# Sample attention of a streaming encoder: queries as weights, 32 columns per pair of heads, in four column groups

## The chip, the cores and the metric

The kernel runs on one core of a Trainium2 chip. The metric is the device time of one execution in microseconds. The time before the change is 3033.25 us, the median of 3 runs (3031.68 to 3037.04). The engines are called PE (TensorE's matmuls), PEld (its weight loads, which overlap the matmuls), DVE (VectorE), ACT (ScalarE), POOL (GpSimd) and SP (SyncE, which issues most of the DMAs).

## What is computed

The reference is one layer of a streaming encoder for a prompt of 2048 frames and for 8 samples (streams) of 16 new frames each. The layer has a mixer (attention and convolution side by side), a cross-attention into 256 memory tokens and a feed-forward network. The change touches the attention of the samples only:

```python
# per sample: 16 queries, 8 heads of 64; keys and values: 256 cached rows and the 16 new ones
s = jnp.einsum("bqhd,bkhd->bhqk", qc, kc, preferred_element_type=jnp.float32) * scale + bias
s = jnp.where(valid[None, None, None, :], s, NEG_INF)
p = jax.nn.softmax(s, axis=-1)
return jnp.einsum("bhqk,bkhd->bqhd", p.astype(vc.dtype), vc)
```

The bias is a learned one per head and relative distance. With 8 heads of 16 queries a sample has 128 rows of scores, each of 272 keys. The two heads 2c and 2c+1 are a pair; their 2 x 64 channels are the 128 channels of block c, for c = 0 to 3.

## The kernel before

The program is built phase by phase: memory keys and values, input projection with the convolution, attention, output projection, cross-attention, feed-forward. A scheduler orders the instructions of each engine from a simulated timeline, so the order on an engine is not that of the code; each engine runs its own list in order. All matmuls of the prompt split an operand into a high and a low part (float32r, types `fp32r` in the profile); those of the samples are plain float32.

`attention()` runs over 128 units (h, t): head h = 0 to 7, tile t = 0 to 15 of 128 queries. In step i it issues the scores of unit i (L861, up to 640 keys, PSUM buffer "s", two of them), then the transposes of the weights of unit i - 4 (L878, PSUM buffer "t", three of them), and every fourth step the values of a quad of units (L891, PSUM buffer "o", a single one). DVE adds the bias and finds the minimum (L793), ACT takes the exponential (L795), ACT and DVE evict the transposes as high and low part (L879 and L880), and ACT and DVE evict the values (L895 and L897).

Between these steps one sample is worked off per head, `sample(s)` with s = h. It is a generator, and `next(fill)` lets it go on by one piece at i = 2, 4, ..., 14 of a head's 16 units, and at every unit at the end of the last head. Its pieces are:

- The DMA loads of the cached keys (L800) and values (L802, "vc", two buffers) and of the new values (L804).
- Two times four transposes of the keys (L812) and their eviction by ACT into kt (L813), each time a piece; then POOL's copy of the 16 new keys into kt (L815), a piece of its own.
- The scores: DVE copies the queries into qb (L820), one of two zeroed tiles of 128 x 4 x 160. Read as 640 columns, its 128-column slice c holds the 32 query columns of pair c at columns 32c to 32c + 31 and zeros elsewhere. Four matmuls (L826), each with such a slice as weights and 272 keys as moving columns, accumulate into the same 128 x 272 of PSUM. Softmax follows (L793, L795, L829, and L830 on POOL).
- Three transposes of the weights (L835), the last of only 16 keys, and their eviction by ACT (L837, L838).
- The values: per pair c, two matmuls with 128 rows of cached values as weights (L844) and one with the 16 new rows (L845); 128 weight columns each time, and 32 moving columns, the weights of the pair's heads. The result is 128 channels x 32, of which DVE copies the two needed parts into attS (L847, L848).

`att_pools()` places the tiles in fixed arenas; fa, fb, sbF and sbR are arenas in SBUF, which the profile and the order show as flexb, sbf, sbr and sbx.

Of the kernel before, what the change touches and what calls it, by code (L numbers as in the profile page):

```python
# [8 lines left out]
F32 = mybir.dt.float32  # L9
# [8 lines left out]
P = 128  # L18
# [12 lines left out]
DEC_S = 16  # L31
# [105 lines left out]
class Build:  # L137
# [611 lines left out]
    def att_pools(self):  # L749
        sbF, sbR, fa, fb = self.sbF, self.sbR, self.fa, self.fb  # L750
        self.attp = (Region().lay(sbF, 34.5, ("kc", 4, 2), ("kt", 4.25, 1), ("pp", 1.5, 1), ("vn", 2, 1))
                     .at("z", 2.5, (fa, [24]), (fb, [0, 2.5, 5]), (fa, [9, 11.5, 14, 16.5]))
                     .lay(fb, 7.5, ("vc", 4, 2), ("nmx", 0.03125, 12), ("sm", 0.03125, 2))
                     .lay(fa, 0, ("qbd", 2.5, 2), ("otmp", 2, 1), ("bs", 1.0625, 1)).lay(fa, 19, ("bt", 2.5, 2))
                     .lay(sbR, 0, ("q20", 8, 1), ("k20", 8, 1), ("kl0", 8, 1), ("q21", 8, 1), ("k21", 8, 1), ("kl1", 8, 1),
                          ("v20", 8, 1), ("ph1", 10, 1), ("pl1", 10, 1), ("v21", 8, 1))
                     .lay(sbR, 88, ("ph0", 10, 1), ("pl0", 10, 1)))
# [25 lines left out]
    def attention(self):  # L783
        nc, A = self.nc, self.A
        ps, pool = self.ps, self.attp
# [4 lines left out]
        def softmax_band(ps, w, bias, sm):  # L790
            z = self.t(pool, [P, W5], F32, "z", 6)
            nmx = self.t(pool, [P, 1], F32, "nmx", 12)
            nc.vector.tensor_tensor_reduce(out=z[:, :w], in0=ps, in1=bias, scale=-1.0, scalar=3e38,  # L793
                                           op0=ALU.add, op1=ALU.min, accum_out=nmx[:, :])
            nc.scalar.activation(z[:, :w], z[:, :w], AF.Exp, bias=nmx[:, :], scale=-1.0, accum_out=sm)  # L795
            return z

        def sample(s):
            kc = self.t(pool, [P, 2, 512], F32, "kc", 2)
            nc.sync.dma_start(kc[:, :, :], A["cache_att_k"][s].rearrange("(b p) d -> p b d", p=P))  # L800
            vc = self.t(pool, [P, 2, 512], F32, "vc", 2)
            nc.sync.dma_start(vc[:, :, :], A["cache_att_v"][s].rearrange("(b p) d -> p b d", p=P))  # L802
            vn = self.t(pool, [DEC_S, 512], F32, "vn", 2)
            nc.sync.dma_start(vn[:, :], self.vsamp[s * DEC_S:(s + 1) * DEC_S, :])  # L804
            yield
            kt = self.t(pool, [P, 4, PAST + DEC_S], F32, "kt", 1)
            for c2 in range(0, 4, 2):
                pt = self.t(ps_t, [P, 2, 2, P], F32, "t")
                for c in range(2):
                    for b in range(2):  # L810
                        cc = slice((c2 + c) * P, (c2 + c + 1) * P)
                        nc.tensor.transpose(pt[:, c, b, :], kc[:, b, cc], self.ident[:, :])  # L812
                nc.scalar.copy(kt[:, c2:c2 + 2, :PAST].rearrange("p c (b k) -> p c b k", k=P), pt[:, :, :, :])  # L813
                yield
            nc.gpsimd.tensor_copy(kt[:, :, PAST:], self.ksamp[:, :, s * DEC_S:(s + 1) * DEC_S])  # L815
            yield
            qb = qbds[s % 2]
            for o in range(2):
                rr = slice(o * DH, (o + 1) * DH)
                nc.vector.tensor_copy(qb[rr, :, o * DEC_S:(o + 1) * DEC_S],  # L820
                                      self.qsamp[rr, :, s * DEC_S:(s + 1) * DEC_S])
            qb = qb[:, :, :].rearrange("p c x -> p (c x)")
            n = PAST + DEC_S
            ps = self.t(ps_s, [P, 2, 512], F32, "s")[:, 0, :n]
            for c in range(4):
                nc.tensor.matmul(ps, qb[:, c * P:(c + 1) * P], kt[:, c, :], start=c == 0, stop=c == 3)  # L826
            sm = self.t(pool, [P, 1], F32, "sm", 2)
            z = softmax_band(ps, n, bs[:, :], sm[:, :])
            nc.vector.reciprocal(sm[:, :], sm[:, :])  # L829
            nc.gpsimd.tensor_scalar(z[:, :n], z[:, :n], sm[:, :], None, ALU.mult)  # L830
            yield
            pt = self.t(ps_t, [P, 3, P], F32, "t")
            for b in range(3):
                w = P if b < 2 else DEC_S
                nc.tensor.transpose(pt[:w, b, :], z[:, b * P:b * P + w], self.ident[:, :])  # L835
            pp = self.t(pool, [P, 3, P], F32, "pp", 1)
            nc.scalar.copy(pp[:, :2, :], pt[:, :2, :])  # L837
            nc.scalar.copy(pp[:DEC_S, 2, :], pt[:DEC_S, 2, :])  # L838
            yield
            po = self.t(ps_o, [P, 4, 32], F32, "o")  # L840
            for c in range(4):
                cc, hc = slice(c * P, (c + 1) * P), slice(c * 32, (c + 1) * 32)
                for b in range(2):
                    nc.tensor.matmul(po[:, c, :], vc[:, b, cc], pp[:, b, hc], start=b == 0, stop=False)  # L844
                nc.tensor.matmul(po[:, c, :], vn[:, cc], pp[:DEC_S, 2, hc], start=False, stop=True)  # L845
            ss = slice(s * DEC_S, (s + 1) * DEC_S)
            nc.vector.tensor_copy(self.attS[:DH, :, ss], po[:DH, :, :DEC_S])  # L847
            nc.vector.tensor_copy(self.attS[DH:, :, ss], po[DH:, :, DEC_S:])  # L848
# [53 lines left out]
        bs = self.t(pool, [P, PAST + DEC_S], F32, "bs")  # L902
# [1 line left out]
            nc.sync.dma_start(bs[h * DEC_S:(h + 1) * DEC_S, :], toep[h][:DEC_S, PAST:2 * PAST + DEC_S])  # L904
        qbds = []
        for _ in range(2):
            qb = self.t(pool, [P, 4, P + 2 * DEC_S], F32, "qbd")
            nc.gpsimd.memset(qb[:, :, :], 0.0)
            qbds.append(qb)
        fill = iter(())  # L910
# [5 lines left out]
        for i in range(n + LV + 1):  # L916
            if i < n:
                h, t = units[i]
                if t == 0:
                    fill = sample(h)  # L920
                if t == 6 and h + 1 < H:
                    heads[h + 1] = self.head_tiles(h + 1)
                    self.head_load(h + 1, heads[h + 1], 0, NPT)
                zq[h, t] = scores(heads[h], t, self.sums[:, t, h:h + 1])
            u = i - LT
            if 0 <= u < n:
                h, t = units[u]
                quads[u // 4] = transp({x: zq.get((h, x)) for x in range(t - t % 4, t + 1)}, t, quads.get(u // 4))
            u = i - LV
            if 0 <= u < n and u % 4 == 3:  # L930
                h, t = units[u]
                values(h, heads[h], t - 3, quads.pop(u // 4))
            if i % NPT and (i % 2 == 0 or i > SLAST):
                next(fill, None)
            if i == n - NPT:
                self.selectors()
            if i in WEIGH:
                for _ in self.weigh(WEIGH.index(i), ps_t, "t"):
                    pass
            if i in (n - 13, n - 11, n - 9, n - 7):  # L940
                next(self.wo_load)
# [760 lines left out]
```

## Time and profile before

| | |
|---|---|
| median of 3 runs | 3033.25 us |
| the profiled execution | 3033.59 us |
| its span, first to last instruction | 3031.8 us |
| its mean granted TensorE clock | 0.987 |
| attention (643 to 917 us) | 274 us, PE busy 261.3, DVE 201.9, ACT 209.6, POOL 23.0 |
| samples' scores, L826 | 64 PE instructions, first at 662.2, last at 906.9 us |
| samples' values, L844 and L845 | 128 and 64 PE instructions, first at 682.5, last at 916.5 us |

The time of the profiled execution holds its span and about 2 us around it. A row of the trace names the engine, the line, the operation, the tile written and those read, then the shapes; `128*128 128x272 f32` on PE is 128 rows by 128 columns of weights and a moving operand of 272 columns. PE's durations run from start to end of one instruction and overlap the next, so the cost of an instruction in a row of many is the distance between starts. Clock 1.00 is full speed.

### The profile page before, as it was taken

What the parts mean: (1) busy time and instruction counts of PE and PEld (TensorE: products, weight loads), DVE (VectorE), ACT (ScalarE), POOL (GpSimd) and SP (SyncE); (2) the same over time, 40 slices, a digit from 0 to 9 for tenths busy, and PEclk for the clock granted to TensorE, in tenths of its full rate; (3) what the DMA queues carried; (4) which work ended last, traced back from release to release, by engine and by line L of the source; (5) the groups of instructions that cost most, each with busy time, mean ns of one, the idle gap of its engine ahead of it and who ended that gap; (6) DMA issues with size and microseconds to landing.
All of it is one profiled execution on the core that took longest, in us unless ns stands there. A gap on an engine that the chain in (4) does not pass through costs nothing.

```text
span 3031.8 us, 45992 instructions
## 1 busy us (share of the span) xinstructions
PE 2949.8 (97%) x16924; PEld 2715.4 (90%) x16924; DVE 2138.1 (71%) x3077; ACT 1357.7 (45%) x2718; POOL 1397.0 (46%) x1304
## 2 busy tenths in 40 slices
PE   8999999979999999999999999999999999999998
PEld 8999999969997888787888999999999999888786
DVE  6696895957775466535357887888788998656655
ACT  4545454757784345323234333433334444433433
POOL 0267495710012234325356655555555776424413
PEclk9999999989999999999999999999999999999999
DMA  8635255557753556324246433544334446756654
GB/s 300 245 110 188 87 161 163 169 142 182 170 145 134 176 183 227 125 66 144 78 167 216 138 133 119 180 161 160 139 130 153 145 139 208 255 172 208 222 196 163
DMA packets 196429, 500.08 MB, mean 165 GB/s; under 512 B 18981, under 2 KB 82989, under 8 KB 187875
## 3 DMA queue, kind: packets, MB, share of 16 engines
q1 hardware_dynamic: 185883, 461.09, 47.3%
q0 software_dynamic: 10320, 36.05, 3.1%
q8 instruction: 133, 2.18, 0.3%
q14 instruction: 93, 0.76, 0.1%
HBM read 365.97 MB, written 141.81 MB: 167 GB/s over the span
## 4 chain that ended last, share of the span: by engine, by line
PE 40%; DMA 3%; DVE 3%; POOL 2%; issue 1%; ACT 1%; SPq 0%; DVEq 0%; POOLq 0%; ACTq 0%
PE psb L285 13%; PE psb L284 13%; PE psb L283 13%; DMA sbf<-in_w_down_dram 1%; PE psb L291 1%; DMA sbf<-x 1%; POOL sbf L1553 1%; DVE sbr L1614 1%; PE psb L1408 1%; DMA sbf<-hn 0%; DVE sbr L1431 0%; POOL sbf L340 0%; DMA hn<-sbf 0%; DVE flexb L1493 0%; DMA sbf<-in_w_gate_dram 0%
## 5 line engine op out<-in xcount | busy, mean ns | idle before, releaser
L283 PE MATMUL psb<-sbr 128*128 128x384 f32 (+3 forms) x2808 | 943.3, 337 | 4.4 <-ACT sbr L1613 1.4
L284 PE MATMUL psb<-sbr 128*128 128x384 f32 (+3 forms) x2356 | 806.8, 343 | 2.7 <-DVE sbr L320 2.4
L285 PE MATMUL psb<-sbr 128*128 128x512 f32 (+3 forms) x1848 | 633.2, 344 | 3.5 <-DVE sbr L1614 3.4
L283 PEld LDWEIGHTS psb<-sbr 128*128 128x128 f32 x2808 | 531.2, 189 | 34.4 <-ACT sbr L1613 2.8
L285 PE MATMUL psb<-sbr,sbx 128*128 128x384 f32 (+2 forms) x1484 | 477.8, 323 | 0.0
L284 PEld LDWEIGHTS psb<-sbr 128*128 128x128 f32 x2356 | 445.8, 189 | 29.8 <-DVE sbr L320 2.7
L285 PEld LDWEIGHTS psb<-sbr 128*128 128x128 f32 x1848 | 348.1, 189 | 33.3 <-DVE sbr L1614 6.6
L291 PE MATMUL psb<-sbr 128*128 128x512 f32 x1200 | 296.1, 395 | 6.4 <-DVE sbr L1019 1.7
L1431 DVE TENSOR_TENSOR sbr<-sbf,sbr 128x512 fp32r<-128x512 f32 x258 | 263.1, 1023 | 39.7 <-ACT sbr L1430 38.8
L1430 ACT CAST sbr<-sbf 128x512 fp32r<-128x512 f32 x258 | 159.3, 620 | 276.9 <-PE psb L284 231.0
L285 PEld LDWEIGHTS psb<-sbr,sbx 128*128 128x128 f32 x1484 | 281.5, 190 | 0.2
L291 PEld LDWEIGHTS psb<-sbr 128*128 128x128 f32 x1200 | 222.8, 189 | 52.9 <-DVE sbr L1019 1.9
L523 DVE SCALAR_TENSOR_TENSOR psb<-sbf,psb 128x768 f32<-128x768 f32 (+1 forms) x290 | 264.3, 911 | 6.2
L1614 DVE TENSOR_TENSOR sbr<-sbf,sbr 128x384 fp32r<-128x384 f32 (+1 forms) x231 | 170.8, 762 | 94.0 <-ACT sbr L1613 92.1
L278 POOL TENSOR_TENSOR sbx<-sbf,sbr 128x1024 fp32r<-128x1024 f32 x60 | 151.6, 2529 | 80.7 <-ACT sbr L277 77.2
L1613 ACT CAST sbr<-sbf 128x384 fp32r<-128x384 f32 (+1 forms) x231 | 111.0, 497 | 168.3 <-PE psb L284 153.7
L1553 POOL TENSOR_TENSOR sbf<-sbf 128x512 f32<-128x512 f32 x77 | 108.0, 1407 | 167.9 <-DMA sbf<-in_w_down_dram 166.1
L533 POOL TENSOR_TENSOR flexb<-flexb,flexb 128x128 f32<-128x128 f32 (+1 forms) x180 | 169.4, 941 | 22.3 <-ACT flexb L532 12.8
L283 PE MATMUL psb<-sbr,sbx 128*128 128x384 f32 (+1 forms) x524 | 170.6, 327 | 1.6 <-ACT sbx L1430 0.9
L1430 ACT CAST sbx<-sbf 128x512 fp32r<-128x512 f32 x153 | 94.7, 621 | 162.4 <-PE psb L284 150.6
L1431 DVE TENSOR_TENSOR sbx<-sbf,sbx 128x512 fp32r<-128x512 f32 x153 | 152.3, 997 | 15.9 <-ACT sbx L1430 15.5
L277 ACT CAST sbr<-sbf 128x1024 fp32r<-128x1024 f32 x98 | 102.7, 1051 | 107.2 <-PE psb L284 57.6
(336 smaller groups left out, 6246.9 us busy)
## 6 DMA issues: line engine op xcount, KB each, us to landing
af<-flexb SPq DMA_DIRECT2D x33, 1344.0 KB, 6.0
sbf<-in_w_down_dram SPq DMA_DIRECT2D x154, 256.0 KB, 3.8
sbf<-af SPq DMA_DIRECT2D x90, 384.0 KB, 3.9
sbf<-in_w_gate_dram SPq DMA_DIRECT2D x66, 512.0 KB, 3.4
sbf<-in_w_up_dram SPq DMA_DIRECT2D x66, 512.0 KB, 3.4
sbf<-x SPq DMA_DIRECT2D x49, 512.0 KB, 3.9
sbf<-in_w_in_dram SPq DMA_DIRECT2D x48, 512.0 KB, 4.1
sbr<-ks SPq DMA_DIRECT2D x28, 512.0 KB, 10.2
```

The source lines that it names most:

```text
L278: self.lo_engine.tensor_tensor(lo[:, :], wf[:, :], hi[:, :].bitcast(F32), ALU.subtract)
L283: nc.tensor.matmul(ps, lh, rh, start=start, stop=False, **kw)
L284: nc.tensor.matmul(ps, lh, rl, start=False, stop=False, **kw)
L285: nc.tensor.matmul(ps, ll, rh, start=False, stop=stop, **kw)
L291: nc.tensor.matmul(y[o], l, r[:, o * 512:(o + 1) * 512], start=start and x == 0, stop=stop and x == 2)
L523: nc.vector.scalar_tensor_tensor(acc if w < CW - 1 else o, src(w), cwt[:, j, w:w + 1], acc, ALU.mult, ALU.add)
L533: nc.gpsimd.tensor_tensor(o, o, v, ALU.add)
L1430: nc.scalar.copy(hs[j][:, :], src[j])
L1431: nc.vector.tensor_tensor(ls[j][:, :], src[j], hs[j][:, :].bitcast(F32), ALU.subtract)
L1553: nc.gpsimd.tensor_tensor(acc[:, :], acc[:, :], q[:, :], ALU.add if s > 0 else ALU.subtract)
L1613: nc.scalar.copy(ch[:, m], a[:, x, m])
L1614: nc.vector.tensor_tensor(cl[:, m], a[:, x, m], ch[:, m].bitcast(F32), ALU.subtract)
```

## The change

The samples' attention is written anew in three places. The scores use as weights only the 32 query columns of a pair (qb shrinks to 128 x 4 x 32), and each of the four matmuls writes its own 32 partitions of PSUM, 32c to 32c + 31, without accumulating over pairs. The values turn the operands round: the weights are the 32 columns of pp, the moving operand is the 128 channels of the pair, and each pair writes its own 32 partitions of a 128 x 128 tile; the blocks b of keys are the outer loop, the pairs the inner one. Since the result now has queries on the partitions, ACT copies it into a new tile osb (L847 of the changed kernel), and in a piece of its own one transpose (L850) puts the channels back on the partitions, in a buffer "t"; the two DVE copies into attS (now L852 and L853) read from there. The number of pieces stays: the second half of the key transposes and POOL's copy are now one piece, and the transpose behind is a new one. So scores, softmax and values come two units earlier in each head.

```diff
-                     .lay(fa, 0, ("qbd", 2.5, 2), ("otmp", 2, 1), ("bs", 1.0625, 1)).lay(fa, 19, ("bt", 2.5, 2))
+                     .lay(fa, 0, ("qbd", 0.5, 2), ("osb", 0.5, 2)).lay(fa, 5, ("otmp", 2, 1), ("bs", 1.0625, 1)).lay(fa, 19, ("bt", 2.5, 2))
...
-                yield
+                if c2 == 0:
+                    yield
             nc.gpsimd.tensor_copy(kt[:, :, PAST:], self.ksamp[:, :, s * DEC_S:(s + 1) * DEC_S])
             yield
...
-            qb = qb[:, :, :].rearrange("p c x -> p (c x)")
             n = PAST + DEC_S
             ps = self.t(ps_s, [P, 2, 512], F32, "s")[:, 0, :n]
             for c in range(4):
-                nc.tensor.matmul(ps, qb[:, c * P:(c + 1) * P], kt[:, c, :], start=c == 0, stop=c == 3)
+                nc.tensor.matmul(ps[c * 32:(c + 1) * 32], qb[:, c, :], kt[:, c, :], start=True, stop=True)
...
-            po = self.t(ps_o, [P, 4, 32], F32, "o")
-            for c in range(4):
-                cc, hc = slice(c * P, (c + 1) * P), slice(c * 32, (c + 1) * 32)
-                for b in range(2):
-                    nc.tensor.matmul(po[:, c, :], vc[:, b, cc], pp[:, b, hc], start=b == 0, stop=False)
-                nc.tensor.matmul(po[:, c, :], vn[:, cc], pp[:DEC_S, 2, hc], start=False, stop=True)
+            po = self.t(ps_o, [P, P], F32, "o")
+            for b in range(3):
+                w, v = (P, vc[:, b, :]) if b < 2 else (DEC_S, vn[:, :])
+                for c in range(4):
+                    hc = slice(c * 32, (c + 1) * 32)
+                    nc.tensor.matmul(po[hc, :], pp[:w, b, hc], v[:, c * P:(c + 1) * P], start=b == 0, stop=b == 2)
+            osb = self.t(pool, [P, P], F32, "osb")
+            nc.scalar.copy(osb[:, :], po[:, :])
+            yield
+            po = self.t(ps_t, [P, 4, 32], F32, "t")
+            nc.tensor.transpose(po[:, :, :].rearrange("p c x -> p (c x)"), osb[:, :], self.ident[:, :])
             ss = slice(s * DEC_S, (s + 1) * DEC_S)
...
-            qb = self.t(pool, [P, 4, P + 2 * DEC_S], F32, "qbd")
+            qb = self.t(pool, [P, 4, 2 * DEC_S], F32, "qbd")
```

The order on PE around the values of sample 1, before. In these rows psb is PSUM, flexb_153 and flexb_157 are the arenas fa and fb, and the shape is that of what is written, partitions x columns; one row may stand for several matmuls.

```order
L878 MATMUL psb<-ident_73,flexb_153 128x128 x4
L844 MATMUL psb<-sbf,flexb_157 128x32 x2
L845 MATMUL psb<-sbf 128x32
L844 MATMUL psb<-sbf,flexb_157 128x32 x2
L845 MATMUL psb<-sbf 128x32
L844 MATMUL psb<-sbf,flexb_157 128x32 x2
L845 MATMUL psb<-sbf 128x32
L844 MATMUL psb<-sbf,flexb_157 128x32 x2
L845 MATMUL psb<-sbf 128x32
L878 MATMUL psb<-ident_73,flexb_157 128x128 x3
```

The same place on PE in the changed kernel, where the band's scores are L866, its transposes L883 and its values L896.

```order
L883 MATMUL psb<-ident_73,flexb_157 128x128 x4
L845 MATMUL psb<-flexb_157,sbf 32x128 x8
L883 MATMUL psb<-ident_73,flexb_157 128x128 x4
L845 MATMUL psb<-sbf 32x128 x4
L883 MATMUL psb<-ident_73,flexb_153 128x128 x4
L866 MATMUL psb<-sbr 128x128 x2
L866 MATMUL psb<-sbr 128x256 x6
L896 MATMUL psb<-sbr 128x128 x2
```

The twelve matmuls now stand in a run of eight (the cached keys) and a run of four (the new keys) with four transposes of the band between them, and the band's own values, which use the same buffer "o", follow twelve matmuls later.

On ACT, the rows of the same sample from the eviction of its weights (L837, L838) on, before.

```order
L837 COPY sbf<-psb 128x256
L838 COPY sbf<-psb 16x128
L795 ACTIVATE flexb_157,sbf<-flexb_157 128x256
L879 CAST sbr<-psb 128x512
L795 ACTIVATE flexb_153,sbf<-flexb_153,flexb_157 128x640
L879 CAST sbx<-psb 128x512
```

And on ACT in the changed kernel, where the casts of the band are L884 and the new copy is L847.

```order
L837 COPY sbf<-psb 128x256
L838 COPY sbf<-psb 16x128
L795 ACTIVATE flexb_153,sbf<-flexb_153,flexb_157 128x640
L884 CAST sbx<-psb 128x512
L795 ACTIVATE flexb_153,sbf<-flexb_153,flexb_157 128x640
L884 CAST sbx<-psb 128x512
L847 COPY flexb_153<-psb 128x128
L884 CAST sbx<-psb 128x512
```

The copy of osb stands behind two exponentials and two casts of the band, and a cast stands behind it. The four score matmuls of a sample (L826) stood together in before in some samples and in two pairs in others; in the changed kernel they stand together for samples 0 and 3 and in two pairs for the other six. Soon after the start of the output projection the orders of the two kernels are the same again, to the end.

## The prediction

> **What bounds the kernel now.** I read the page's head first, for the share of each engine. PE is TensorE's matmul row, DVE is VectorE, ACT is ScalarE.
>
> ```profile
> span 3031.8 us, 45992 instructions
> PE 2949.8 (97%) x16924; PEld 2715.4 (90%) x16924; DVE 2138.1 (71%) x3077; ACT 1357.7 (45%) x2718; POOL 1397.0 (46%) x1304
> ```
>
> PE is busy for 97% of the span, but a share is a mean over stages. The change touches the attention alone, so the second view is the busy time by stretch, for its steady part (676 to 911 us) and for five stretches of 5 us in it. The columns are length, then busy time and instructions of PE, PEld (weight loads), DVE, ACT, POOL, then the granted TensorE clock, the DMA share and GB/s.
>
> ```profile
> 676.00:911.00 235.00, 233.68 (x1564) 219.35 (x1562) 181.22 (x435) 186.36 (x430) 19.92 (x30) 0.94 0.63 161
> ...
> 781.00:786.00 5.00, 5.00 (x42) 4.84 (x41) 4.38 (x12) 4.95 (x15) 0.00 (x0) 1.00 0.75 170
> 786.00:791.00 5.00, 5.00 (x37) 4.63 (x36) 3.59 (x10) 3.27 (x9) 0.00 (x0) 1.00 1.00 222
> ...
> 806.00:811.00 5.00, 5.00 (x40) 4.89 (x39) 5.00 (x13) 4.87 (x11) 0.96 (x1) 1.00 0.07 26
> ...
> 816.00:821.00 5.00, 5.00 (x31) 4.57 (x30) 3.06 (x9) 2.36 (x7) 0.00 (x0) 0.81 0.98 195
> 821.00:826.00 5.00, 5.00 (x21) 4.61 (x22) 2.62 (x7) 2.26 (x5) 0.29 (x2) 0.51 1.07 233
> ```
>
> Over the 235 us PE idles 1.3 us; ACT (186.4) and DVE (181.2) have a fifth to spare. But the spare time is not spread evenly: at 781 and 806 us ACT or DVE is full too (4.95 and 5.00 of 5), and they rest where a sample's values run (786 to 791) and where the clock is halved (821 to 826). So PE sets the time, with ACT and DVE close behind.
>
> The mean clock of 0.94 is the second finding. The timeline of PE shows one sample's values (columns: start, length, then the group; the difference of two starts is what a group costs), and the clock of eight stretches of 3.4 us, one behind the values of each sample, says where the clock goes.
>
> ```profile
> 785.98 0.53 PE L844 MATMUL psb<-sbf,flexb 128*128 128x32 f32 x4
> 786.44 0.40 PE L845 MATMUL psb<-sbf 16*128 16x32 f32 x2
> 786.77 0.63 PE L844 MATMUL psb<-sbf,flexb 128*128 128x32 f32 x4
> 787.33 0.40 PE L845 MATMUL psb<-sbf 16*128 16x32 f32 x2
> 787.67 0.63 PE L844 MATMUL psb<-sbf,flexb 128*128 128x32 f32 x4
> ...
> 789.46 0.66 PE L878 MATMUL psb<-ident,flexb 128*128 128x128 f32 x4
> ```
>
> ```profile
> 685.90:689.30 3.40, 3.40 (x15) 3.27 (x15) 1.46 (x5) 0.40 (x1) 0.00 (x0) 0.51 0.65 193
> 720.10:723.50 3.40, 3.40 (x18) 3.33 (x18) 1.96 (x7) 1.11 (x3) 0.00 (x0) 0.50 1.05 255
> 755.10:758.50 3.40, 3.40 (x14) 3.00 (x14) 1.61 (x5) 1.09 (x2) 0.00 (x0) 0.50 1.05 246
> 789.50:792.90 3.40, 3.40 (x26) 3.27 (x26) 2.84 (x8) 2.20 (x5) 0.29 (x2) 1.00 1.03 251
> 820.70:824.10 3.40, 3.40 (x14) 2.99 (x14) 1.25 (x4) 0.59 (x1) 0.00 (x0) 0.50 1.08 241
> 856.60:860.00 3.40, 3.40 (x17) 3.31 (x16) 2.93 (x7) 2.99 (x6) 0.00 (x0) 0.50 0.96 207
> 891.00:894.40 3.40, 3.40 (x17) 3.25 (x17) 2.85 (x9) 2.08 (x4) 0.00 (x0) 0.53 0.78 264
> 916.70:920.10 3.40, 3.40 (x25) 3.19 (x25) 3.15 (x11) 2.43 (x6) 0.00 (x0) 1.00 0.38 154
> ```
>
> Six of eight are at half clock. The values feed 32 columns behind weights of 128, so for 3.48 us (785.98 to 789.46) the array mostly waits for weights, and the clock drops right behind them. At a mean of 0.94, 0.06 x 235 = 14 us of PE time are lost.
>
> **The change part by part.** All sums are made against the profiled execution, 3033.6 us (span 3031.8), which is 0.3 us from the median of the runs, 3033.25. A measurement of this kernel can tell about 0.2%, 6 us, from no change.
>
> *Costs now.* Two more places of PE's timeline give the prices: a sample's scores (L826) between band work, and its transposes (L835).
>
> ```profile
> 706.07 1.03 PE L878 MATMUL psb<-ident,flexb 128*128 128x128 f32 x8
> 706.94 2.00 PE L826 MATMUL psb<-sbf,flexb 128*128 128x272 f32 x8
> 708.58 0.60 PE L861 MATMUL psb<-sbr 128*128 128x256 f32 x2
> ...
> 713.74 0.71 PE L861 MATMUL psb<-sbr 128*128 128x256 f32 x4
> 714.29 0.60 PE L878 MATMUL psb<-ident,flexb 128*128 128x128 f32 x4
> 714.73 0.49 PE L835 MATMUL psb<-ident,flexb 128*128 128x128 f32 x3
> 714.97 1.41 PE L861 MATMUL psb<-sbr 128*128 128x384 f32 x6
> ```
>
> ```profile
> L826 PE MATMUL psb<-sbf,flexb x64: 392/393/497, 662.2 to 906.9; 128*128 128x272 f32 x64
> ```
>
> 64 instructions for 8 x 4 matmuls: a plain float32 matmul is two instructions. The scores take 1.64 us for 8, 0.205 us each, by 272 moving columns. A transpose (128 columns) takes 0.87/8 = 0.109 us. In the values four instructions of L844 take 0.56 us and two of L845 0.34: with c per instruction and s per change between 128 and 16 rows, 4c + s = 0.56 and 2c + s = 0.34, so c = 0.11 and s = 0.12 us.
>
> *Values.* Again 24 instructions (12 matmuls), now with 32 weight columns and 128 moving ones. By the score's row 128 columns stream in 0.205 x 128/272 = 0.096 us, by the transposes' in 0.109; I take 0.109. No row shows two column groups at once. If nothing overlaps: 24 x 0.109 + 2 changes of rows (0.24) = 2.86 us, 0.62 less than now. If all four groups run together: the run of 8 matmuls is 4 instructions deep in each group and the run of 4 is 2 deep, 6 x 0.109 + 0.24 = 0.90, 2.58 less. I take a value between: both instructions of a matmul go to one group back to back, and PE starts in order as in all rows above, so the second instruction of one matmul can run with the first of the next, and no more. n matmuls then take n + 1 slots: (9 + 5) x 0.109 + 0.24 = 1.77 us, 1.71 less.
>
> *Scores.* The order shows them in one run of four in 2 samples and in two runs of two in 6. No overlap: 1.64 as now. Half: 5 slots x 0.205 = 1.03, or 2 x 3 x 0.205 = 1.23, mean 1.18, 0.46 less. Full: 0.41 or 0.82, mean 0.72, 0.92 less.
>
> *The transpose behind*, one more: 0.11 us. Net per sample: half 1.71 + 0.46 - 0.11 = 2.06, times 8 = 16.5 us. None: 0.51, 4.1 us. Full: 3.39, 27 us.
>
> *Changes of the array's shape.* The third transpose of L835 loads 16 columns instead of 128, and the three still take 0.24 us with what follows, as any others: a narrower load costs nothing, so only the change of rows (0.12) is in my sum. The Trainium skill, "TensorEngine Tiling (Array Packing)", Key Properties, says that a change of tiling mode drains the array, whichever way it changes. By that, each run of column groups would cost two drains, about 7 per sample instead of the 2 counted; at 0.12 us the forecast would be about 5 us later, 3014. Only the row change agrees with it here.
>
> *The clock.* Bursts of 1.77 us that stream without a pause, in two pieces, replace 3.48 us of starved array; half as long and busier, they should not trip the clock, so I credit the whole 14 us.
>
> *ACT.* One copy of 128x128 out of PSUM per sample:
>
> ```profile
> L710 ACT COPY sbf<-psb x20: 245/270/314, 576.3 to 645.3; 128x128 f32<-128x128 f32 x20
> ```
>
> 0.27 us each, 1.9 in the stretch: ACT's work is 186.4 + 1.9 = 188.3. PE's time there falls to 235 - 14 - 7 x 2.06 = 206.6, so ACT's share rises from 79% to 91% and the lulls in which it caught up are gone. What is late next is therefore ACT (and DVE at 88%), and PE waits for buffers. Lower bound 0. Upper bound: ACT never above 85%, its share between two samples at full clock, 29.03 us of 34:
>
> ```profile
> 776.00:810.00 34.00, 34.00 (x246) 32.47 (x244) 28.76 (x74) 29.03 (x69) 2.64 (x6) 1.00 0.67 166
> ```
>
> 188.3/0.85 = 221.5, 15 us of waiting. Since ACT and DVE do reach 4.95 and 5.00 of 5 without PE standing, I take 6, nearer the lower end.
>
> *The rest.* The smaller qbd clears, the two DVE copies and the POOL product remain what they were, and POOL is busy 19.9 of 235 us. The queue of SP keeps its loads; the buffers of vc are free earlier, not later. These I cost at nothing.
>
> Sum: 14 + 16.5 - 6 = 24.5 us, 3033.6 - 24.5 = **3009 us**.
>
> **The rivals.**
>
> *The column groups run one after the other* (the change doesn't do what it says). PE gains 14 + 4.1, ACT's share is 188.3/217.4 = 87%, and I let half as much waiting stand, 3 us: 3019 us. For it: no row shows two matmuls in one array.
>
> *All four groups overlap.* PE gains 14 + 27; then PE's 235 - 14 - 23.7 = 197 stands against ACT's 188.3, 96%, and I take 11 us of waiting: 3003 us. Against it stands the pairing of instructions. For it: the Trainium skill, "TensorE: Matmul & The Clock Gate", Measured speedup vs the span model, gives 2.38 times for three column groups that start about 4 ns apart.
>
> *The clock still drops.* If a column of 32 counts as an idle array, the 14 us stay and a little less waiting comes: 3033.6 - 16.5 + 2 = 3019. Against it: the bursts are half as long.
>
> *The ACT copy holds the values' buffer.* "o" is one buffer, and the order shows the next band values close behind the sample's. Between them stand four transposes (0.44 us) and those eight (0.55/4 = 0.14 us each by the rows at 713.74 and 714.29, two of them narrower), 1.4 us in all, in which ACT must reach the copy. Behind the copy on ACT stand casts that DVE waits for. ACT was up to 2.0 us late for DVE:
>
> ```profile
> DVE sbr L880 <- ACT sbr L879: 7.3, 12, 2.0
> ```
>
> 2.0 + 0.27 - 1.4 = 0.9 us, 8 times: 7 us, 3016.
>
> *Slower: the loads of the narrow weights are not hidden.* Now each load runs under the matmul before it.
>
> ```profile
> L835 PEld LDWEIGHTS psb<-ident,flexb x24: 88/139/141, 677.4 to 911.3; 128*128 128x128 f32 x16, 128*16 128x16 f32 x8
> L835 PE MATMUL psb<-ident,flexb x24: 270/272/330, 677.5 to 911.4; 128*128 128x128 f32 x16, 128*16 128x128 f32 x8
> ```
>
> If in column groups each must end before its matmul starts, and the matmul before the next load, an instruction costs 0.09 + 0.27 us in the values and 0.09 + 0.39 in the scores: 24 x 0.36 + 8 x 0.48 = 12.5 us per sample in place of 5.1, 59 us with 8 samples, and the 14 us of clock stay lost: 3033.6 + 59 + 1 = 3094. It decides from 0.12 us of exposure per instruction (30.5 us over 256). Against it: the 16-column load of L835 is hidden.
>
> **How the numbers follow.** Half overlap, 3009: 0.46. One after the other, 3019: 0.22. Full, 3003: 0.12. Clock still drops, 3019: 0.07. Buffer "o", 3016: 0.05. Exposed loads, 3094: 0.08. The range of 2999 to 3025 holds the first five cases with their bounds, but for their edges. Serial groups and a dropping clock together would give 3030, so I move 0.08 of the first five to no change: faster 0.84, same 0.08, slower 0.08.
>
> **What would show it.** Half overlap: from the first L845 of a sample to what follows its runs of 8 and 4, about 1.0 and 0.65 us; runs of 2.4 us and more would mean no overlap. The clock behind the values reads 1.00. ACT's share in the attention is about 0.9, with PE waits on ACT and DVE of some 6 us. The forecast is wrong if the clock stays at 0.94, if ACT holds PE for 15 us or more, or if the start of the mixer's output gives the gain back.

## The result and the profile after

| | before | after |
|---|---|---|
| median | 3032.47 us (4 runs, 3030.72 to 3037.04) | 3014.07 us (4 runs, 3012.76 to 3015.97) |
| ratio, 95% interval | | 0.9939 [0.9923, 0.9955] |
| the profiled execution, span | 3033.59, 3031.8 us | 3012.76, 3011.0 us |

The changed kernel is faster, by 18.4 us in the medians and 20.8 us in the profiled spans. The forecast was 3009 us, 24.5 us of gain. On the same chip as the last experiments the changed kernel, run again, came out at 0.9944 [0.9932, 0.9956].

First the head of the page of after: PE still leads with 97%.

```profile
span 3011.0 us, 46007 instructions
PE 2925.7 (97%) x16932; PEld 2676.2 (89%) x16932; DVE 2126.8 (71%) x3077; ACT 1354.8 (45%) x2726; POOL 1392.6 (46%) x1304
```

Then the busy time of the steady stretch, with the columns as before: length, PE, PEld, DVE, ACT, POOL, granted clock, DMA share, GB/s.

```profile
676.00:911.00 235.00, 227.93 (x1706) 198.33 (x1706) 194.73 (x466) 199.10 (x467) 24.04 (x32) 1.00 0.65 168
```

The clock is 1.00 in place of 0.94. PE now idles 7.1 of 235 us (1.3 before), and ACT works 85% of the stretch (79% before).

The timeline of PE around one sample's values and around its scores, in two pieces here, shows the column groups at work.

```profile
678.42 0.64 PE L845 MATMUL psb<-flexb,sbf 128*32 128x128 f32 x16
678.99 0.66 PE L883 MATMUL psb<-ident,flexb 128*128 128x128 f32 x4
679.58 0.42 PE L845 MATMUL psb<-sbf 16*32 16x128 f32 x8
679.93 0.86 PE L866 MATMUL psb<-sbr 128*128 128x384 f32 x4
...
699.32 0.65 PE L826 MATMUL psb<-sbf,flexb 128*32 128x272 f32 x4
699.90 0.66 PE L883 MATMUL psb<-ident,flexb 128*128 128x128 f32 x4
...
759.83 0.67 PE L826 MATMUL psb<-sbf,flexb 128*32 128x272 f32 x8
760.42 0.66 PE L883 MATMUL psb<-ident,flexb 128*128 128x128 f32 x4
```

Sixteen instructions of the values take 678.99 - 678.42 = 0.57 us, the eight of 16 rows 0.35: 0.92 us for the sample in place of 3.48. A score run of two matmuls (x4) takes 0.58 us, one of four (x8) 0.59: the four groups run together, and a run that holds only two of them takes as long as one that holds four.

The records of single instructions behind these rows say what a run costs beside its streaming (start in us, and ns to the start before):

```
699.113        L812  transpose, 128 columns of weights
699.315   202  L826  pass 1, first group
699.322     7  L826  pass 1, second group
699.569   247  L826  pass 2
699.576     7  L826  pass 2
699.899   323  L883  transpose, 128 columns of weights
700.064   165  L883
700.173   109  L883
```

A transpose usually costs 109 ns until the next start, and a pass over 272 columns 229 in the scores before. Going into column groups costs 202 - 109 = 93 ns more, coming out 323 - 229 = 94, and the first transpose behind it 165 - 109 = 56: about 0.24 us a run.

To compare kernels I also use three marks of the trace: the first score matmul of head 0, that of head 1, and the matmul that stands 300 behind the first of the output projection (L291), called its 300th here, which stands behind all of the attention.

| us | head 0 | heads 1 to 7 | head 0's start to the projection's 300th | half clock in heads 1 to 7 |
|---|---|---|---|---|
| before | 38.3 | 241.6 | 372.4 | 27.3 |
| after | 42.5 | 216.1 | 351.0 (-21.4) | 0.0 |

("Heads 1 to 7" ends at the last score matmul.) Seven heads gain 25.5 us, and the first loses 4.2. Only the whole stretch to the 300th encloses the same work in both: sample 0's values start at 682.46 us before, behind head 1's first scores (681.56), and at 678.42 after, ahead of them (684.59).

That stretch can be taken apart in three: the time for which PE is idle; the time lost to half clock, an estimate, half of the time for which PE is busy there (in before the transposes L878 start 213 ns apart at half clock and 109 at full); and the rest, PE's own work.

| us, head 0's start to the projection's 300th | PE idle | lost to half clock | PE's own work |
|---|---|---|---|
| before | 19.5 | 20.1 | 332.8 |
| after | 22.5 | 11.1 | 317.3 |

So the gain of 21.4 us is 15.5 of PE's own work and 9.0 of clock, less 3.0 of idle time. The five kernels below that ask of PE just what after does have 317.0 to 317.8 us of own work, so that column can be read to about 1 us. The other two vary from one execution to the next: the changed kernel, run again, idles 26.9 us and loses 6.6 to the clock.

Two rows of after show where the first head stands: SP's queue issues the samples' bias, eight transfers, over 12.6 us, and PE waits for the softmax that needs it.

```profile
656.97 12.59 SPq L909 DMA_DIRECT2D flexb<-toep  x8
```

```profile
671.73 1.01 PE L866 MATMUL psb<-sbr 128*128 128x384 f32 x2 [5.05 <-DVE flexb L793]
```

Before, PE waited 3.44 us at this place, up to 672.04. The bias came no earlier, and the sample's scores, two units earlier now, wait longer for it. But the wait at the key transposes (L812) of the same head fell from 5.1 to 3.3 us, and over head 0 PE idles 11.4 us in place of 11.2. What makes head 0 longer is the clock, an estimated 6.4 us lost in place of 3.3, and the values of sample 0, which stand in it now (own work 24.8 us in place of 23.8).

### The profile page after: what moved, and what is told of

Read it like the earlier page. It is cut to its first block, busy times and chain, and to the rows that moved or that the text cites. A ratio compares the mean times of both kernels' runs of the same rounds, so it can differ in the third digit from the quotient of the medians.

```text
span 3011.0 us, 46007 instructions
## 1 busy us (share of the span) xinstructions
PE 2925.7 (97%) x16932; PEld 2676.2 (89%) x16932; DVE 2126.8 (71%) x3077; ACT 1354.8 (45%) x2726; POOL 1392.6 (46%) x1304
## 4 chain that ended last, share of the span: by engine, by line
PE 38%; DMA 4%; POOL 3%; issue 3%; DVE 2%; ACT 1%; SPq 0%; DVEq 0%; POOLq 0%; ACTq 0%
PE psb L285 12%; PE psb L284 12%; PE psb L283 12%; DMA sbf<-in_w_down_dram 2%; POOL sbf L1558 1%; PE psb L291 1%; DMA sbf<-x 1%; PE psb L1413 1%; DVE sbr L1619 0%; POOL sbf L340 0%; DVE sbr L1436 0%; DMA sbf<-in_w_gate_dram 0%; DMA sbf<-hn 0%; DMA hn<-sbf 0%; DVE flexb L1498 0%
## 5 line engine op out<-in xcount | busy, mean ns | idle before, releaser
L285 PEld LDWEIGHTS psb<-sbr 128*128 128x128 f32 x1848 | 348.4, 189 | 33.4 <-DVE sbr L1619 6.9
L291 PE MATMUL psb<-sbr 128*128 128x512 f32 x1200 | 297.8, 397 | 4.3 <-POOL sbr L1271 1.5
L1436 DVE TENSOR_TENSOR sbr<-sbf,sbr 128x512 fp32r<-128x512 f32 x258 | 262.6, 1021 | 39.8 <-ACT sbr L1435 38.9
L291 PEld LDWEIGHTS psb<-sbr 128*128 128x128 f32 x1200 | 223.6, 190 | 50.5 <-POOL sbr L1271 1.9
L533 POOL TENSOR_TENSOR flexb<-flexb,flexb 128x128 f32<-128x128 f32 (+1 forms) x180 | 167.1, 929 | 21.7 <-ACT flexb L532 12.1
L1436 DVE TENSOR_TENSOR sbx<-sbf,sbx 128x512 fp32r<-128x512 f32 x153 | 154.5, 1012 | 17.9 <-ACT sbx L1435 17.5
L277 ACT CAST sbr<-sbf 128x1024 fp32r<-128x1024 f32 x98 | 102.5, 1050 | 108.2 <-PE psb L284 56.1
```

What stands on the lines that cost most here:

```text
L285: nc.tensor.matmul(ps, ll, rh, start=False, stop=stop, **kw)
L291: nc.tensor.matmul(y[o], l, r[:, o * 512:(o + 1) * 512], start=start and x == 0, stop=stop and x == 2)
L533: nc.gpsimd.tensor_tensor(o, o, v, ALU.add)
L1436: nc.vector.tensor_tensor(ls[j][:, :], src[j], hs[j][:, :].bitcast(F32), ALU.subtract)
```

## Experiments

The theory that went into the first ones: the groups overlap fully, the clock no longer drops, and ScalarE (ACT) and VectorE (DVE) are now nearly as late as TensorE (PE), which is why not all of PE's saving shows. The main rival: PE alone still sets the time. The ratios are against runs of the kernel before on the same chip.

| kernel | ratio [95%] | head 0 | heads 1 to 7 | to the projection's 300th | PE idle | lost to half clock | PE's own work |
|---|---|---|---|---|---|---|---|
| values alone | 0.9951 [0.9936, 0.9966] | 40.1 | 222.2 | 354.1 | 22.6 | 11.7 | 319.8 |
| scores alone | 0.9996 [0.9983, 1.0008] | 39.1 | 230.3 | 369.4 | 18.1 | 24.0 | 327.2 |
| before, values in halves | 0.9995 [0.9985, 1.0005] | 39.8 | 230.4 | 367.8 | 18.5 | 13.1 | 336.2 |
| after, group by group | 0.9946 [0.993, 0.9962] | 42.6 | 217.6 | 353.6 | 23.9 | 12.5 | 317.2 |
| after, more PE | 0.9959 [0.9946, 0.9971] | 38.8 | 229.2 | 358.1 | 20.0 | 6.9 | 331.3 |
| after, more ACT | 0.9948 [0.9934, 0.9962] | 38.5 | 219.3 | 351.6 | 24.0 | 10.5 | 317.1 |
| after, more DVE | 0.995 [0.9937, 0.9964] | 42.4 | 220.0 | 353.7 | 27.0 | 9.7 | 317.0 |
| after, one bias transfer | 0.9934 [0.9922, 0.9947] | 40.4 | 215.4 | 348.0 | 21.7 | 8.9 | 317.4 |
| after again | 0.9944 [0.9932, 0.9956] | 42.0 | 220.3 | 351.3 | 26.9 | 6.6 | 317.8 |
| after, scores in one run | 0.9984 [0.9975, 0.9993] | 43.0 | 230.4 | 365.6 | 33.4 | 11.8 | 320.4 |
| before, one bias transfer | 0.9982 [0.9973, 0.9991] | 37.9 | 244.7 | 371.8 | 17.5 | 21.9 | 332.4 |
| three edits together | 0.9929 [0.9917, 0.9941] | 37.4 | 219.1 | 347.1 | 26.3 | 6.0 | 314.9 |

The ratio is of many executions, the other columns of the profiled one; the last three split its stretch to the 300th as above.

**Values alone.** The scores stay as before, with the large padded queries.

```diff
-                nc.tensor.matmul(ps[c * 32:(c + 1) * 32], qb[:, c, :], kt[:, c, :], start=True, stop=True)
+                nc.tensor.matmul(ps, qb[:, c * P:(c + 1) * P], kt[:, c, :], start=c == 0, stop=c == 3)
```

> The change's values (column groups, copy, transpose behind), but the scores as before. Theory (groups overlap fully, the clock no longer drops, and ScalarE and VectorE are nearly as late as TensorE, so that more TensorE time saved no longer counts fully): the mean clock in 676 to 911 us is 1.00, and the time is 15 to 19 us below before, most of the changed kernel's 18.4. Rival (TensorE alone sets the time and what it saves counts one for one): the scores' 8 x 0.9 = 7 us are missing, 11 us below before. The clock tells whether the values' starved burst was what dropped it: with the scores left as they were it must still stay at 1.00.

**Scores alone.** The change's scores, with the values of before, in the pieces of before.

> The change's scores (column groups, small padded queries), but the values as before. Theory: the values' burst of 3.5 us is untouched, so the clock stays at about 0.94 in 676 to 911 us and TensorE alone sets the time; the scores' run falls from 1.64 to about 0.7 us, 8 x 0.9 = 7 us: 4 to 8 us below before. Rival (a change of the array's shape costs as much as the overlap brings): within 2 us of before. Rival (scores at 32 columns are what kept the clock up): clock 1.00 and over 15 us below before.

For both, busy time between 686 and 895 us, before, with the values alone and with the scores alone.

```profile
686.00:895.00 209.00, 208.28 (x1387) 195.85 (x1387) 163.10 (x393) 164.11 (x381) 13.72 (x26) 0.93 0.69 172
```

```profile
686.00:895.00 209.00, 201.66 (x1500) 182.09 (x1498) 174.85 (x419) 178.71 (x418) 19.36 (x29) 0.99 0.70 174
```

```profile
686.00:895.00 209.00, 208.44 (x1411) 191.29 (x1411) 164.37 (x396) 166.52 (x387) 16.12 (x27) 0.94 0.67 170
```

With the values alone the clock is 0.99 and the gain 14.8 us by the ratio (0.0049 x 3030): the starved values were what dropped the clock. That is a little under the 15 to 19 expected, and the ratio's interval, 10 to 19 us, holds the rival's 11 too. With the scores alone the clock stays at 0.94, as expected, but the gain expected at 4 to 8 us is not there: 1 us by the ratio, within its interval none, and 3.0 us up to the projection's 300th matmul. PE's own work did fall by 5.6 us, but the clock took 3.9 of it back, 3.5 of that behind the last head (in heads 1 to 7 it costs 13.7 us in both). A split score run of two and two costs 2 x 0.58 us and some 0.15 more twice at the neighbours, 1.46 of 8 x 229 ns = 1.83 us before (the prediction's 1.64 ends at the start of the band's scores, 28 ns behind the last pass); a single run costs 0.74. With four samples of each kind here that makes 5.8 us, and 5.6 came. The two parts add up: 18.3 + 3.0 us up to the projection's 300th matmul, 21.4 for both together.

**Values in halves.** The kernel before, with the values issued two pairs of heads at a time.

```diff
+            for c2 in range(0, 4, 2):
+                po = self.t(ps_o, [P, 2, 32], F32, "o")
...
+                if c2 == 0:
+                    yield
```

> The kernel before, its values untouched in form but issued in two halves with band work between (two pairs of heads each, 1.7 us of starved array at a time instead of 3.5; two more copies of 0.2 us on VectorE per sample, one step of the transposes' moved up as in the change). Theory (a starved burst of over 3 us halves the clock): the clock rises from 0.94 to 0.99 or more in 676 to 911 us, and the time is 10 to 14 us below before: then over half of the change's gain is the clock's. Rival (the drop goes by the starved time in sum, not by the length of a burst): clock about 0.94, time within 3 us of before.

```profile
686.00:895.00 209.00, 207.81 (x1441) 191.98 (x1441) 166.35 (x414) 169.59 (x391) 16.11 (x27) 1.00 0.68 173
```

The clock went to 1.00 here, and half clock in heads 1 to 7 fell from 27.3 to 3.4 us: the length of the starved burst is what counts, 3.5 us drop the clock (in six of eight samples) and 1.8 do not. Heads 1 to 7 became 11.2 us shorter, as the theory has it. But only 4.6 us (372.4 to 367.8) were left up to the projection's 300th matmul, and the median did not move; the profiled execution, 3024.84 us, is the fastest of twelve, whose median is 3031.17. The parts say where the rest went. In heads 1 to 7 the clock gives back 12.0 us, but it takes 3.1 more in head 0 and 2.0 more behind the last head, and PE's own work is 3.4 us longer. So the burst's length decides the clock in heads 1 to 7, but 14 us there are not 14 us at the end; why the clock falls at other places instead I did not settle.

**Group by group.** The values' eight matmuls in the other order.

```diff
-            for b in range(3):
...
-                for c in range(4):
+            for b, c in [(b, c) for c in range(4) for b in range(2)] + [(2, c) for c in range(4)]:
```

> The changed kernel with the values' eight matmuls of 128 rows ordered group by group (both blocks of one pair of heads, then the next pair), not block by block. If TensorE starts in order, four passes of one group stand in a row and only the last can run beside the next group's first: 13 slots of 0.109 us, 1.4 us instead of 0.57 for the run, 8 x 0.85 = 7 us more of TensorE's time, of which the theory (ScalarE and VectorE nearly as late) lets 2 to 5 us reach the end; a TensorE that alone sets the time lets all 7. Rival (each group has a queue of its own): the run stays at about 0.57 us and the time that of the changed kernel.

```profile
677.79 0.67 PE L844 MATMUL psb<-flexb,sbf 128*32 128x128 f32 x16
678.38 0.66 PE L882 MATMUL psb<-ident,flexb 128*128 128x128 f32 x4
```

The run takes 0.59 us (0.57 in after), and the time is that of the changed kernel. PE's own work is the same too (317.2 and 317.3 us). An engine that starts its instructions in the order of the code would have needed 1.4. The records have four starts 13 or 14 ns apart, then 95 ns or less to the next four (in after 6 to 8, then 90 to 112): each column group works off its own instructions, and the order in which the code names them costs nothing. The records don't name the group, so this is read from the times; the doubled distance fits the edit, which puts four instructions of a group ahead of the next group's first in place of two, some 3.3 ns each.

**More PE, more ACT, more DVE.** Each adds 2 us a sample to one engine of the changed kernel.

```diff
+                for _ in range(10 if b == 0 else 1):
...
+            for _ in range(10):
                 nc.tensor.transpose(po[:, :, :].rearrange("p c x -> p (c x)"), osb[:, :], self.ident[:, :])
```

```diff
+            for _ in range(4):
+                nc.scalar.copy(scr[:, :], z[:, :P])
...
+            for _ in range(4):
+                nc.scalar.copy(scr[:, :], osb[:, :])
```

(with `nc.vector.tensor_copy` for DVE)

> The changed kernel with 18 transposes of 0.109 us repeated in each sample (nine beside the first of the softmax's, nine beside the one behind the values; what they compute is the same again): 2.0 us of TensorE per sample, 15.7 us in all, against the changed kernel's 18.4 us below before. Theory (all three engines are nearly equally late in the samples' stretch, TensorE waits some 25 to 30 us of 235 there): a part fills waits and 7 to 12 us of it reach the end, 6 to 11 below before. Rival (TensorE still sets the time alone): all 15.7, 3 below before. Rival (ScalarE sets the time alone): under 3, 15 or more below before.

> The changed kernel with eight copies of 128x128 repeated on ScalarE in each sample (four behind the softmax's evictions, four at the sample's end, into a tile that nobody reads): 0.25 us each, 2.0 per sample, 16 us in all. Theory (three engines nearly equally late): 6 to 11 us reach the end, 7 to 12 below before. Rival (TensorE alone sets the time, as before the change): under 3 us, 15 or more below before. Rival (ScalarE alone): 14 to 16, 2 to 4 below before.

> The same eight copies of 128x128 per sample on VectorE in place of ScalarE, 0.2 to 0.3 us each, 13 to 19 us in all. Theory (three engines nearly equally late): 5 to 10 us reach the end, 8 to 13 below before. Rival (TensorE alone, or ScalarE alone): under 3, 15 or more below before.

The busy time between 686 and 895 us of the changed kernel, of more ACT and of more DVE:

```profile
686.00:895.00 209.00, 201.99 (x1527) 175.51 (x1526) 173.13 (x425) 181.07 (x427) 19.46 (x29) 1.00 0.69 175
```

```profile
686.00:895.00 209.00, 202.06 (x1520) 176.57 (x1519) 174.98 (x419) 190.41 (x476) 19.42 (x29) 0.99 0.69 175
```

```profile
686.00:895.00 209.00, 199.81 (x1489) 173.25 (x1487) 181.88 (x469) 178.17 (x416) 19.35 (x29) 0.98 0.68 172
```

The theory of three engines equally late falls. ACT at 190 of 209 us, 91%, costs nothing that can be told: up to the projection's 300th matmul 16 us more of ACT cost 0.6 us, as much of DVE 2.7, where 6 to 11 and 5 to 10 were expected, and the ratios are those of the changed kernel. But PE does not set the time alone either. Of 15.7 us more of PE 7.1 arrive at that mark (4.5 to 6 by the ratios), the foot of the theory's 7 to 12, and the kernel is 12.4 us below before, where a PE that sets the time alone would leave 3. PE's own work grew by 14.0 us there; its idle time fell by 2.5 and the loss to the clock by 4.3. So work on PE counts in part, and work on ACT and DVE hardly. (The 25 to 30 us of waiting in the expectation are near the sum of the weight loads' waits; PE itself idles 7.1 of the 235 us.) A caution goes with all three: the intervals of the three ratios overlap, and the scheduler rebuilds every engine's list when the code changes, so a few us of each number belong to the order.

**One bias transfer.** All 128 rows in one DMA.

```diff
-        for h in range(H):
-            nc.sync.dma_start(bs[h * DEC_S:(h + 1) * DEC_S, :], toep[h][:DEC_S, PAST:2 * PAST + DEC_S])
+        nc.sync.dma_start(bs[:, :], bass.AP(toep[0].tensor, toep[0].offset + PAST,
+                                            [[5 * P * P, H], [5 * P, DEC_S], [1, PAST + DEC_S]]))
```

> The changed kernel with the samples' bias fetched by one transfer over all 128 partitions in place of eight, which the queue issued over 12.6 us, the last landing at about 671 us, with VectorE waiting 5.3 us for it and TensorE 5.05 in the first head. Theory (this wait and the 6.8 us of half clock behind it are the 4 us by which the first head grew): the wait is under 1 us, the first head takes 36 to 39 us in place of 42.5, and the time falls 4 to 7 us further, 22 to 25 below before. Rival (what the first head waits for comes in anyway with the loads that stand in the queue behind it, or the gain is given back before the mixer's output): within 2 us of the changed kernel.

> The kernel before with the bias in one transfer. Before, VectorE waited 4.3 us for the eight transfers and TensorE 3.4. Theory (the wait belongs to the bias transfers and not to the change): 2 to 4 us below before. Rival (before the change other work covers it): within 1 us of before.

SP's queue and PE's wait with one transfer in the changed kernel:

```profile
656.42 0.65 SPq L908 DMA_DIRECT2D flexb<-toep  x1
```

```profile
669.83 0.62 PE L866 MATMUL psb<-sbr 128*128 128x384 f32 x2 [3.00 <-DVE flexb L793]
```

The issue takes 0.65 us in place of 12.59, but the bias is there only 2 us earlier: 656.42 to 669.3 is still 13 us, with the heads' and samples' loads ahead of it in the same queue. Its packets run from 666.3 to 668.6 us, and the DMA engines are busy all the time up to there (a share of 1.00 from 656.4 on). So the wait shrinks from 5.05 to 3.00, not under 1, and head 0 from 42.5 to 40.4; 3.0 us are left at the projection's 300th matmul, less than the 4 to 7 expected. By the ratio the kernel is 20.0 us below before, which is within the rival's 2 us of the changed kernel, so the two can't be told apart. In the kernel before, the same edit gives 0.9982, 5.5 us, more than the 2 to 4 expected, of which its profile shows 0.6 up to that mark: that it helps is measured, where is open.

**After again, scores in one run, and three edits together.** The order 2, 3, 0, 1 puts the four score matmuls in one run in seven of eight samples, in place of two:

```diff
-            for c in range(4):
+            for c in (2, 3, 0, 1):
                 nc.tensor.matmul(ps[c * 32:(c + 1) * 32], qb[:, c, :], kt[:, c, :], start=True, stop=True)
```

> The changed kernel as it is, as the measure for the other three on the same chip: 14 to 21 us below before.

> The changed kernel with the four score matmuls in the order 2, 3, 0, 1, which makes the first of them wait for the second half of the keys, so that all four stand in one run in seven samples in place of two. A run of two takes 0.58 us, as long as a run of four, and each run seems to cost another 0.15 us at the change of the array's shape: 5 runs fewer, 3.7 us of TensorE. Theory (TensorE sets the time, some half to all of what it saves reaches the end): 2 to 4 us below the changed kernel. Rival (time that TensorE saves now goes into waits for ScalarE and VectorE): within 1 us of it.

> The changed kernel with the bias in one transfer, the scores in one run, and the two evictions of the softmax's transposes swapped on ScalarE, so that the values' 16-row block stands right behind the two of 128 rows in every sample (one change of the array's shape and back, some 0.2 us, less per sample). Theory (TensorE sets the time): 3.4 us of the bias, 3 of the scores, 1 to 1.5 of the values, 6 to 8 us below the changed kernel. Rival (waits take what TensorE saves): no more than the bias's 3 to 4 us below it.

One run was expected to gain 2 to 4 us and lost 14.3 up to the projection's 300th matmul (0.9984 against 0.9944). Against the changed kernel run again, 6.5 of them are idle time of PE, 5.2 clock and 2.6 PE's own work, which did not fall. The busy time between 686 and 895 us shows PE standing still:

```profile
686.00:895.00 209.00, 193.24 (x1427) 167.28 (x1425) 166.59 (x401) 169.96 (x397) 16.04 (x27) 0.99 0.69 171
```

All three engines are less busy than in the changed kernel, since less of the work falls into the 209 us. The waits of the same stretch name the place (engine, who it waits for, us in total, times, longest); first the changed kernel, then the one with one run.

```profile
DVE sbf L902 <- ACT flexb L900: 10.1, 8, 1.9
ACT flexb L900 <- PE psb L896: 6.4, 9, 1.2
PE psb L866 <- DVE flexb L793: 3.3, 8, 0.9
```

```profile
DVE sbf L902 <- ACT flexb L900: 16.1, 10, 2.0
ACT flexb L900 <- PE psb L896: 14.0, 16, 1.4
PE psb L866 <- DVE flexb L793: 5.6, 10, 1.5
PE psb L883 <- DVE sbr L885: 3.7, 7, 1.1
PE psb L896 <- DVE sbx L885: 3.6, 5, 0.8
```

ACT stands at the eviction of the band's values (L900) until PE has done them, DVE at the sum behind it (L902) until ACT has, and the softmaxes and casts queued behind these two come late, for which PE waits in turn. The lists differ from the changed kernel's in over 400 of ACT's 2726 rows and over 600 of DVE's 3077, though only four matmuls changed places in the code. That the waits are these is shown; that the order of the lists is their cause, and not the later scores themselves, is argued, by the last kernel, which also has one run and does not lose: 0.9929, 347.1 us up to the mark, 4.2 less than the changed kernel on the same chip. It has the one transfer, the one run and this swap:

```diff
-            nc.scalar.copy(pp[:, :2, :], pt[:, :2, :])
             nc.scalar.copy(pp[:DEC_S, 2, :], pt[:DEC_S, 2, :])
+            nc.scalar.copy(pp[:, :2, :], pt[:, :2, :])
```

```profile
695.63 0.67 PE L826 MATMUL psb<-sbf,flexb 128*32 128x272 f32 x8
...
704.87 0.64 PE L845 MATMUL psb<-flexb,sbf 128*32 128x128 f32 x16
705.45 0.42 PE L845 MATMUL psb<-sbf 16*32 16x128 f32 x8
```

It does what it says: one run of scores, one of values with the 16-row block right behind. It has the lowest ratio of all, but the intervals overlap; of 6 to 8 us expected some 4 came, no more than the bias's share, so by the time the rival of this expectation stands. By the parts 2.9 of them are PE's own work (317.8 to 314.9), less than the 4 to 4.5 us expected of scores and values.

The traces of this kernel and of the changed one run again show a wait that no expectation named. The copies of the output projection's weights (L277) stand in ACT's list among the casts of the last heads, and ACT stands at such a copy until a transfer has landed, 4.7 us here and 5.1 in the changed kernel run again (2.2 at most in the changed kernel's first profile). The band's casts behind it come late, and PE stands for 4.9 and 3.9 us in one piece. From the changed kernel run again, between 686 and 895 us:

```profile
ACT sbr L277 <- DMA sbf<-in_w_out_dram: 7.2, 2, 5.1
PE psb L896 <- ACT sbx L884: 4.7, 2, 3.9
```

## Why the prediction was right, and where it was not

**What bounds the kernel** was read rightly: PE first, before and after. But added work on PE arrives only in part, 7.1 of 15.7 us.

**The clock.** The burst as the cause, and 1.00 behind the shorter ones, hold, and heads 1 to 7 gain the 14 us (an estimated 13.7). But the sum looked at that stretch alone: head 0 loses 3.1 us more to half clock than before, and what stands behind the last head 1.7 more. 9.0 us are left of the 14; this is the term of the sum that was most off.

**Overlap.** This step failed: "both instructions of a matmul go to one group back to back, and PE starts in order as in all rows above". The four groups run beside each other whatever the order. The values take 0.92 us, where full overlap had been priced at 0.90 and half at 1.77. The rows above it, all of one full array, could not show it. In the scores six samples have two runs of two at 0.58 each; with the two samples in one run that is 1.02 us on average (full 0.72, half 1.18). The rival with all four groups, given 0.12, was the right mechanism. The Trainium skill's "TensorE: Matmul & The Clock Gate", Measured speedup vs the span model, on which it leant, puts about 4 ns between the starts of matmuls that run side by side; the trace agrees in kind, with 6 to 8 ns for four groups, and its 2.38 times for three groups no run here shows.

**Changes of the array's shape.** "A narrower load costs nothing, so only the change of rows (0.12) is in my sum" failed too. L835 narrows a load inside the same mode; a column group changes the mode, and each run costs about 0.24 us around it. The Trainium skill, "TensorEngine Tiling (Array Packing)", Key Properties, says that a change of mode drains the array, and the trace agrees with 93 and 94 ns for going in and out. Six samples have two runs of values and two have one, and each has one or two of scores; only the two changes of rows were counted. That the estimate made by that page, 3014, is the time measured is luck in part: it added small changes to a half overlap that was not there.

**The stall.** PE's idle time rose by 5.8 us in the stretch (1.3 to 7.1), as the 6 us had it, and by 3.0 over all up to the projection's 300th matmul, since PE waits less behind the last head. The reason given, ACT's share, is wrong: 91% of ACT cost nothing. That the waits come from the order in the lists is argued, not shown.

**The sum** was 14 of clock, 16.5 of PE's work and 6 of waiting, 24.5 us. Up to the projection's 300th matmul the parts measured are 9.0, 15.5 and 3.0, 21.5 us. That 15.5 is so near 16.5 is luck. By the rows, with 0.149 us (93 + 56) for each run beside its own time, the values cost 0.92 + 0.30 = 1.22 us in six samples and 1.07 in two in place of 3.48, the scores 1.46 in six and 0.74 in two in place of 1.83, and the transpose behind 0.11: 17.5 + 4.4 = 21.9 us less in eight samples. 6.4 us of this did not come. With the values alone 13.0 came of 17.4, with the scores alone 5.6 of 5.8, so most of it is missing at the values; what takes it stays open.

**The rest** held a term that I put at nothing. "The queue of SP keeps its loads", but scores that come two units earlier meet a bias that comes no earlier, and PE waits 1.6 us longer for it. The wait for the keys gave that back, though, so the first head's 4.2 us are the clock's and sample 0's values, as above.

The other rivals are out. Loads are not exposed (3094): the narrow ones lie under the passes, as 0.57 us for 16 of them shows. The "o" buffer is not held: in after's trace no instruction waits for the copy of osb (L847). The clock did not stay down: half clock in heads 1 to 7 went from 27.3 to 0.0 us. Nor do the groups run one after the other, which was priced at 2.86 us for a sample's values; they take 0.92.

## What to carry to other kernels

Small matmuls that use 32 columns of the array can run four at once, whatever their order, but each stay in that mode costs about as much as two transposes; so price the runs, not the matmuls, and keep such matmuls in one run where that holds up no other engine. An engine at 91% is not a bound for that: add work to it and see, before counting its waits against the gain. Where a scheduler writes the order, a small edit reshuffles every engine's list, and one such edit lost 14.3 us here; compare marks that enclose the same work, split the time between them into waits, clock and work, and try two variants before believing one.

## What the runs showed of the hardware

- Four float32 matmuls in four column groups take as long as two, 0.59 and 0.58 us for 272 columns, and their starts are 6 to 8 ns apart; a stay in column groups costs 93 ns going in, 94 out, and 56 at the next transpose.
- PE at 100% busy by its records still fell to half clock behind six of eight bursts of 3.5 us with 32 moving columns on 128-column weights; 1.8 us at a time left the clock at 1.00 in six of the seven heads 1 to 7.
- One transfer in place of eight cut the issue from 12.59 to 0.65 us, and the data came only 2 us sooner: its packets began at 666.3 us, behind the loads ahead of it in the queue.
